# An encoder kernel: Fourier of the prompt in half the banks, opening loads in halves, later rows' norm queued behind the first rows

## Chip, core and metric

The kernel runs on one core of a Trainium2 chip. The metric is the device time of one execution in microseconds (us).

## What is computed

Two layers of a gated mixer block run over 512 positions of a prompt and 1024 of a sample, all of width 1024, in fp32. Each layer has windowed attention (8 heads), a Fourier mixing of four channel groups, gates, two merges, and an embedding that is added through a gate:

```python
for i in range(DEPTH):                       # 2 layers
    hn = rmsnorm(h, ln1[i])
    z = hn @ w_in[i]                         # 1024 -> 4352
    q, k, v, ga, uf, gf, mga, mgf = jnp.split(z, SPLIT_IDX, axis=-1)
    ...
    a = band_attention(q, k, v, sink[i]) * jax.nn.silu(ga)
    f = fourier_mix(uf, w_fmix[i]) * jax.nn.silu(gf)   # 4 groups of 128: Re(FFT2), then a 128x128 map
    merged = jax.nn.sigmoid(mga) * (a @ w_ao[i]) + jax.nn.sigmoid(mgf) * (f @ w_fo[i])
    h = h + merged @ w_out[i]
    gate = jax.nn.sigmoid(rmsnorm(h, ln_pg[i]) @ w_pg[i])
    h = h + (p[i] @ w_pe[i]) * gate
return rmsnorm(h, ln_f)
```

The prompt and the sample use the same weights.

## The kernel before

**Products.** Positions are cut into three chunks of 512 columns: chunk 0 is the prompt, chunks 1 and 2 (the pair) the sample. An activation or weight tile is split into a high part, rounded to fp32r by ScalarE (line 86), and a low part, the rest, by VectorE or GpSimd (line 87); `halves` and `hi_lo` do it. A product is then three matmuls (lines 98 to 100: high by high, high by low, low by high), each of 512 columns. The pair's input projection uses seven products in place of eight (line 233).

**Order.** The generators at the end of the kernel interleave a main stream of matmuls with a side stream (`run`). The order in the program is only a priority: a planner at compile time simulates all engines (line 1129, `schedule_with_timeline_sim=True`) and fixes, for every engine, the order in which its instructions are issued. On the chip each engine goes through that list in order and waits where an input, a buffer or a bank is not there yet. `pinned` (line 381) keeps an instruction in program order against others so marked; `normed` (line 352) doesn't.

**Stages.** First `embed(0)` multiplies the embedding input `p` by `w_pe` for all three chunks and stores the result, with `first_prompt` beside it, which loads the prompt, takes its RMS norm and makes the parts of the first projection. Then, in each layer: `project_prompt` (34 outputs of 24 matmuls, weights from `Weights`) with, beside it, the norm and the parts of the pair (`pair_normed`: rows 0 and 1 with `pinned`, rows 2 and 3 with `normed`; each row norms four tiles, then `pair_parts` makes seven split tiles of them), the prompt's attention and the prompt's Fourier part `fourier(l, 0)`; `project_pair` with the sample's attention; `merge` of the prompt with the sample's Fourier part `fourier(l, 1)` beside it; and `merge` of the pair. The last layer ends with the final norm of the pair.

**Weights.** `Weights` loads tile i+3, splits tile i+2 and hands out tile i at each step. Its `engs` names the engines of the two low parts of each tile: VectorE for the first layer's projection, GpSimd for the stream that serves both merges and the next layer's projection. In that stream tiles 0 to 23 are the prompt's merge, 24 to 47 the pair's, and those from 48 on the next projection (or, in the last layer, a second pass of gate weights).

**Banks.** PSUM has the tags mm (3 banks), sc (2), o (1) and misc (2). In `fourier(l, 0)` each group takes four banks in turn (misc, o, misc, misc) for the first transform (lines 850 to 859), each 256 columns wide, evicted by ScalarE (line 858) and VectorE (line 859), and four (sc, sc, misc, misc) for the second (line 878), of which 128 or 130 columns are used.

**Loads.** SyncE's queue issues nearly all loads. In `embed` each of the two `w_pe` tiles and each `p` tile is one transfer of 512 KB; `ln` and `ident` are loaded ahead of them.

## Time and profile before

| | us |
|---|---|
| median of 3 runs | 2255.76 (2255.22 to 2256.32) |
| the profiled execution, its own time | 2258.37 |
| its span, first to last instruction | 2255.9 |

| engine | busy, us | share of the span |
|---|---|---|
| TensorE matmul (PE) | 2182.3 | 97% |
| TensorE weight load (PEld) | 1809.5 | 80% |
| VectorE (DVE) | 1460.9 | 65% |
| ScalarE (ACT) | 1088.5 | 48% |
| GpSimd (POOL) | 558.0 | 25% |

An engine's busy time leaves out its waits and the instructions that only issue transfers. Matmuls are pipelined: a busy TensorE is not one at its peak, so stalls and the granted clock are looked for by stretch. L87 is line 87; in a tile's name the number of the buffer is left out; "out<-in" names what an instruction writes and reads.

### The profile page before, as it was taken

The page shows a single profiled execution, that of the slowest core. Times are in us where ns is not written, and L with a number is a line of the kernel's source. Part 1 is how long each engine was busy: PE and PEld are TensorE (multiplying, and loading weights), DVE is VectorE, ACT ScalarE, POOL GpSimd, SP SyncE. Part 2 cuts the span into 40 slices and gives each one's busy share as a digit, 9 for nine tenths or more (in the row PEclk, how much of TensorE's full clock was granted, in tenths as well). Part 3 has the DMA queues.
Part 4 walks back from the last instruction along what each step waited for, and adds up shares of the span by engine and source line. Part 5 has one row for each costly group of instructions (what it writes and reads, how often), then busy time and mean ns, then how long its engine had stood idle before and what let it go on. Part 6 is the DMA issues. An engine that isn't in the chain of part 4 may idle for free. (4 is left out here: it accounts for less than half of the span.)

```text
span 2255.9 us, 30026 instructions
## 1 busy us (share of the span) xinstructions
PE 2182.3 (97%) x10176; PEld 1809.5 (80%) x10176; DVE 1460.9 (65%) x2703; ACT 1088.5 (48%) x2340; POOL 558.0 (25%) x399
## 2 busy tenths in 40 slices
PE   8899999999999989999999999999999999999996
PEld 7777777788888878888888778787888888788885
DVE  5866657677667775464557564756766676864466
ACT  5477433466665454223324854336666644512342
POOL 0201100000004553312524253100000145641181
PEclk9899999999999999999999999999999999999998
DMA  7655544445448564731445554444444574653232
GB/s 279 230 181 167 188 140 163 148 137 166 150 133 294 189 236 174 251 103 51 146 158 188 173 178 167 151 165 137 143 141 158 194 270 159 225 201 117 83 118 98
DMA packets 240537, 380.69 MB, mean 169 GB/s; under 512 B 21120, under 2 KB 95488, under 8 KB 240384
## 3 DMA queue, kind: packets, MB, share of 16 engines
q1 hardware_dynamic: 233472, 366.19, 48.0%
q10 hardware_dynamic: 6912, 12.59, 1.5%
q8 instruction: 80, 1.31, 0.2%
q14 instruction: 73, 0.60, 0.1%
HBM read 270.17 MB, written 108.53 MB: 168 GB/s over the span
## 5 line engine op out<-in xcount | busy, mean ns | idle before, releaser
L233 PE MATMUL mm<-act,act 128*128 128x512 f32 x2856 | 695.2, 394 | 10.8 <-DVE scr L250 6.4
L233 PEld LDWEIGHTS mm<-act,act 128*128 128x128 f32 x2856 | 531.7, 188 | 123.4 <-issue 8.0
L98 PE MATMUL mm<-act,act 128*128 128x512 f32 x1408 | 559.1, 397 | 19.8 <-DVE scr L585 7.6
L100 PE MATMUL mm<-act,act 128*128 128x512 f32 x1408 | 556.5, 396 | 2.7 <-POOL act L87 1.3
L99 PE MATMUL mm<-act,act 128*128 128x512 f32 x1408 | 555.3, 394 | 0.0
L87 POOL TENSOR_TENSOR act<-act,act 128x512 fp32r<-128x512 f32 x284 | 404.1, 1448 | 547.2 <-ACT act L86 481.2
L86 ACT CAST act<-act 128x512 fp32r<-128x512 f32 x574 | 330.3, 619 | 225.1 <-DMA act<-in_w_af 60.7
L98 PEld LDWEIGHTS mm<-act,act 128*128 128x128 f32 x1408 | 267.8, 190 | 73.7 <-ACT act L86 13.0
L100 PEld LDWEIGHTS mm<-act,act 128*128 128x128 f32 x1408 | 267.5, 190 | 60.6 <-DVE act L87 3.5
L99 PEld LDWEIGHTS mm<-act,act 128*128 128x128 f32 x1408 | 268.1, 190 | 53.3
L87 DVE TENSOR_TENSOR act<-act,act 128x512 fp32r<-128x512 f32 x290 | 212.1, 763 | 47.1 <-ACT act L86 45.9
L87 DVE TENSOR_TENSOR act<-scr,act 128x512 fp32r<-128x512 f32 x256 | 193.7, 777 | 58.0 <-ACT act L86 56.3
L748 POOL TENSOR_TENSOR scr<-scr,scr 128x512 f32<-128x512 f32 x24 | 33.5, 1396 | 768.5 <-DVE scr L745 767.1
L86 ACT CAST act<-scr 128x512 fp32r<-128x512 f32 (+1 forms) x260 | 152.8, 615 | 144.4 <-DVE scr L410 69.0
L322 ACT ACTIVATE scr<-act 128x512 f32<-128x512 f32 x105 | 65.1, 631 | 233.7 <-DVE act L569 145.9
L87 DVE TENSOR_TENSOR act<-misc,act 128x512 fp32r<-128x512 f32 x132 | 88.1, 686 | 75.5 <-ACT act L86 75.1
L707 DVE CUSTOM_DVE_ANT_0 act<-sc,mask_sb,nsink_sb 128x384 f32<-128x384 f32 (+1 forms) x192 | 104.0, 569 | 46.4 <-PE sc L699 43.3
L710 ACT ACTIVATE act<-act,stat 128x385 f32<-128x385 f32 (+1 forms) x192 | 110.5, 578 | 43.9 <-DVE stat L707 43.4
L86 ACT CAST act<-misc 128x512 fp32r<-128x512 f32 x132 | 73.8, 586 | 106.8 <-PE misc L734 104.9
L98 PE MATMUL sc<-act,act 128*128 128x512 f32 (+1 forms) x292 | 111.1, 381 | 0.0
L100 PE MATMUL sc<-act,act 128*128 128x512 f32 (+1 forms) x292 | 110.6, 379 | 0.0
L99 PE MATMUL sc<-act,act 128*128 128x512 f32 (+1 forms) x292 | 110.5, 379 | 0.0
(207 smaller groups left out, 2642.8 us busy)
## 6 DMA issues: line engine op xcount, KB each, us to landing
act<-in_w_in SPq DMA_DIRECT2D x136, 256.0 KB, 4.5
act<-in_w_in SPq DMA_DIRECT2D x68, 512.0 KB, 4.8
gt<-scr SPq DMA_DIRECT2D x96, 256.0 KB, 2.3
scr<-gt SPq DMA_DIRECT2D x96, 256.0 KB, 5.3
act<-in_w_pg SPq DMA_DIRECT2D x80, 256.0 KB, 3.8
act<-in_w_af SPq DMA_DIRECT2D x64, 256.0 KB, 5.3
act<-in_w_out SPq DMA_DIRECT2D x64, 256.0 KB, 5.4
pl<-scr ACTq DMA_DIRECT2D x48, 256.0 KB, 2.5
```

What stands on the lines that cost most here:

```text
L86: S.copy(hi, src)
L87: lo_eng.tensor_tensor(lo, src, f(hi), op=ALU.subtract)
L98: PE.matmul(out, wh, xh, start=i == 0, stop=False)
L99: PE.matmul(out, wh, xl, start=False, stop=False)
L100: PE.matmul(out, wl, xh, start=False, stop=i == n - 1)
L233: PE.matmul(bank, w, v, start=first and k == 0 and n == 0, stop=k == 3 and n == 2, skip_group_check=True)
L322: S.activation(sq, h, AF.Square)
L707: V.tensor_tensor_reduce(out=pr[:, :W], in0=sc[:, :W], in1=msk, scale=-0.125, scalar=nsink_sb[:, l, head : head + 1], op0=ALU.add, op1=ALU ...
L710: S.activation(pr, pr, AF.Exp, bias=nmx[:, e], scale=-1.0, accum_out=rs[:, e])
L748: G.tensor_tensor(a2, a2, gate, op=ALU.mult)
```

## The change

Six edits are made together:

- `embed`: the two `w_pe` tiles are loaded in halves, with the halves of `p`'s first tile between them, ahead of `ln` and `ident`; all low parts are made by VectorE (before, half of the `w_pe` ones by GpSimd); in layer 0 its products go round six banks in place of three.
- Opening: the first two weight tiles of the first projection are loaded behind the prompt's `x`, and split after some of the prompt's parts, in a generator `opening` that runs beside `embed(0)`.
- `pair_normed`: the norm of rows 2 and 3 is queued on VectorE behind the last subtraction of the row before.
- `fourier(l, 0)`: both halves of a first transform share one bank, and are evicted together; the four sums of the second transform share two banks.
- `Weights`: the engines of the low parts depend on the tile's place in the stream: VectorE for tiles 0 to 23, GpSimd for 24 to 47, VectorE from 48 on.

```diff
--- before.py
+++ after.py
@@ -106,12 +106,7 @@
             pass
 
 
-    def const(src, shape, name):
-        t = cpool.tile(shape, F32, tag=name, name=name)
-        SY.dma_start(t, src)
-        return t
-
-    ln_sb = const(ln, [P, 5, KD], "ln_sb")
+    ln_sb = cpool.tile([P, 5, KD], F32, tag="ln_sb", name="ln_sb")
     mean_sb = cpool.tile([P, 1], F32, tag="mean_sb", name="mean_sb")
     V.memset(mean_sb, 1.0 / D)
     ident_sb = cpool.tile([P, P], F32, tag="ident_sb", name="ident_sb")
@@ -160,7 +156,7 @@
         def split(self, i):
             if i < len(self.sources):
                 self.w[i] = []
-                for r, eng in zip((slice(0, 4), slice(4, 8)), self.engs):
+                for r, eng in zip((slice(0, 4), slice(4, 8)), self.engs[min(i // 24, 2)]):
                     t = wt([P, 2, 4, P], F32R)
                     hi_lo(t[:, 0], t[:, 1], self.raw[i][:, r], eng)
                     self.w[i] += [(t[:, 0, k, :], t[:, 1, k, :]) for k in range(4)]
@@ -371,7 +367,7 @@
         yield
         x["B21"].append(two(halves(b21, V)))
         yield
-        V.tensor_tensor(b21, b21, t2, op=ALU.subtract)
+        x["last"] = V.tensor_tensor(b21, b21, t2, op=ALU.subtract).ins
         x["T4"].append(two(halves(b21, V)))
         yield
         x["B22"].append(two(halves(b22, V)))
@@ -386,7 +382,11 @@
             hs = [[tile(i, kk) for i in range(2)] for kk in (k, k + 4)]
             for j in range(2):
                 for i in range(2):
-                    (pinned if k < 2 else normed)(hs[j][i], k + 4 * j, gain, rbs[i])
+                    if k < 2:
+                        pinned(hs[j][i], k + 4 * j, gain, rbs[i])
+                    else:
+                        with tc.issue_after(x["last"]):
+                            normed(hs[j][i], k + 4 * j, gain, rbs[i])
                 yield
             yield from pair_parts(x, hs[0][0], hs[0][1], hs[1][0], hs[1][1])
 
@@ -628,18 +628,25 @@
             SY.dma_start(raw, p[l, c].rearrange("k p t -> p k t"))
             return raw
 
-        ws, raws = {}, []
+        ws, raws = {}, [big([P, 2, T]) for _ in range(2)]
+        raws_p = [big([P, 2, T])]
+
         for k in range(2):
-            raws.append(big([P, 2, T]))
-            SY.dma_start(raws[-1], w_pe[l, k].rearrange("p (i d) -> p i d", i=2))
-            if k == 0:
-                raws_p = [load(0), load(1)]
-        yield
+            SY.dma_start(raws[k][:, 0, :], w_pe[l, k, :, 0:T])
+            SY.dma_start(raws_p[0][:, k, :], p[l, 0, k])
+        for k in range(2):
+            SY.dma_start(raws[k][:, 1, :], w_pe[l, k, :, T:])
+        if l == 0:
+            SY.dma_start(ln_sb, ln)
+            SY.dma_start(ident_sb, ident)
+        raws_p.append(load(1))
+        yield
+        ts = []
         for i in range(2):
             for k in range(2):
-                ws[k, i] = halves(raws[k][:, i, :], V if k else G)
-                if i + k == 0:
-                    ts = [halves(raws_p[0][:, j, :], V) for j in range(2)]
+                ws[k, i] = halves(raws[k][:, i, :], V)
+                if i == 0:
+                    ts.append(halves(raws_p[0][:, k, :], V))
         yield
         for c in range(NCH):
             parts = [two(t) for t in ts]
@@ -650,7 +657,7 @@
                 if m == 4 and c + 1 < NCH:
                     ts = [halves(raws_p[c + 1][:, k, :], V) for k in range(2)]
                 o = slice(m % 4 * P, m % 4 * P + P)
-                out = pst("mm")
+                out = any_ps() if l == 0 else pst("mm")
                 mm3(out, [(ws[k, m // 4][:, 0, o], ws[k, m // 4][:, 1, o]) for k in range(2)], parts)
                 a = scr()
                 S.copy(a, out)
@@ -847,14 +854,18 @@
             for i in range(2):
                 a = scr()[:, : 2 * n * P]
                 for par in range(2):
-                    pm = pst(("misc", "o", "misc")[(2 * i + par) % 3])
+
+                    if s or par == 0:
+                        pm = pst(("misc", "o", "misc")[(2 * i + par) % 3] if s else "misc")
                     for t in range(n):
-                        j, lo = 2 * t * P, 2 * t * P + par
+                        j, lo = (2 * t if s else 2 * par) * P, 2 * t * P + par
                         uh, ul = (z[:, lo : lo + 2 * P - 1 : 2] for z in us[i])
                         PE.matmul(pm[:, j : j + 2 * P], uh, cw[i][:, :, gs], start=True, stop=False)
                         PE.matmul(pm[:, j : j + P], ul, cw[i][:, 0, gs], start=False, stop=True)
-                    pv = pm[:, : 2 * n * P].rearrange("p (t h d) -> p t h d", t=n, h=2)
-                    av = a[:, par * n * P : (par + 1) * n * P].rearrange("p (t d) -> p t d", t=n)
+                    if s == 0 and par == 0:
+                        continue
+                    pv = pm.rearrange("p (t h d) -> p t h d", t=2, h=2)
+                    av = (a[:, par * n * P : (par + 1) * n * P] if s else a).rearrange("p (t d) -> p t d", t=2)
                     S.copy(av, pv[:, :, 1])
                     V.tensor_tensor(av, av, pv[:, :, 0], op=ALU.add)
                 yield
@@ -875,7 +886,11 @@
             if g < 3:
                 folded = fold(u)
             yield
-            acc = [pst("sc"), pst("sc"), pst("misc"), pst("misc")]
+            if s:
+                acc = [pst("sc"), pst("sc"), pst("misc"), pst("misc")]
+            else:
+                b0, b1 = pst("sc"), pst("sc")
+                acc = [b0, b0[:, 2 * P :], b1, b1[:, 2 * P :]]
             for i in range(4):
                 a, par = ab[i // 2], i % 2
                 wx = [(a[:, 0, (par * n + t) * P :][:, :P], a[:, 1, (par * n + t) * P :][:, :P]) for t in range(n)]
@@ -976,14 +991,21 @@
     def w_ins(l):
         return [w_in[l, m] for m in range(NMT)]
 
-    SY.dma_start(ident_sb, ident)
     parts, tiles, rbs = [], [], []
-    first = first_prompt(parts)
-    run(embed(0), [(first, 1, 0.7)])
-    late_constants()
-    ws = Weights(w_ins(0), (V, V))
-    for _ in ws.start():
-        pass
+    ws = Weights(w_ins(0), ((V, V),) * 3)
+
+    def opening():
+        first, weights = first_prompt(parts), ws.start()
+        next(first)
+        next(weights)
+        late_constants()
+        yield
+        for n, _ in enumerate(first):
+            if n == 12:
+                next(weights, None)
+            yield
+
+    run(embed(0), [(opening(), 1, 0.7)])
     for l in range(DEPTH):
         last = l == DEPTH - 1
         xs = {n: [] for n in ("B11", "T2", "T1", "T3", "B21", "T4", "B22")}
@@ -1008,7 +1030,7 @@
         ])
         for _ in pair_made(xs, l, range(3, 4)):
             pass
-        ws = Weights(streams(l) + ([] if last else w_ins(l + 1)), (G, G))
+        ws = Weights(streams(l) + ([] if last else w_ins(l + 1)), ((V, V), (G, G), (V, V)))
         fx = {c: [] for c in range(NCH)}
         run(project_pair(l, xs, pairs, ws.start()), [
             (chain(attention(l, PAIR, True), mixed(0, range(8), fx)), 14 * 5, 1.4),
```

## Rows read from the trace of the kernel before

**Rows 1.** The page, part 1: busy us, share of the span, instructions.
```profile
PE 2182.3 (97%) x10176; PEld 1809.5 (80%) x10176; DVE 1460.9 (65%) x2703; ACT 1088.5 (48%) x2340; POOL 558.0 (25%) x399
```

**Rows 2.** Waits of PE, whole span: total us, times, longest us.
```profile
PE misc L328 <- DVE scr L323: 8.2, 3, 6.3
```

**Rows 3.** Stretches: busy us (instructions) by engine, PEclk granted, DMA share, GB/s.
```profile
15.00:40.00 25.00, 25.00 (x117) 20.80 (x116) 15.52 (x33) 17.69 (x34) 0.00 (x0) 1.00 0.67 235
...
104.04:111.69 7.65, 6.53 (x15) 4.66 (x16) 6.93 (x12) 4.09 (x8) 0.00 (x0) 0.50 0.90 275
234.60:241.40 6.80, 6.80 (x24) 6.12 (x25) 4.56 (x23) 3.25 (x12) 0.59 (x1) 0.50 0.31 112
831.90:838.70 6.80, 3.46 (x8) 2.81 (x9) 5.88 (x9) 1.89 (x3) 1.32 (x1) 0.50 0.11 42
1340.50:1347.30 6.80, 6.36 (x17) 5.18 (x18) 3.31 (x15) 2.09 (x8) 2.07 (x3) 0.50 0.20 74
```

**Rows 4.** Timeline of the opening: start, us, engine, line, tiles [idle before, releaser].
```profile
0.74 0.39 SPq L111 DMA_DIRECT2D ln_sb<-in_ln  x1
...
1.65 0.42 SPq L634 DMA_DIRECT2D act<-in_w_pe  x1
...
5.21 0.62 ACT L86 CAST act<-act 128x512 fp32r<-128x512 f32 x1 [3.19 <-DMA act<-in_w_pe]
6.71 1.14 ACT L86 CAST act<-act 128x512 fp32r<-128x512 f32 x2 [0.89 <-DMA act<-in_p]
...
7.38 1.65 PE L98 MATMUL mm<-act,act 128*128 128x512 f32 x3 [7.38 <-ACT act L86]
```

**Rows 5.** Timeline of DVE while the pair's rows are normed, layer 0.
```profile
94.06 2.73 DVE L352 SCALAR_TENSOR_TENSOR act<-act,ln_sb,scr 128x512 f32<-128x512 f32 x4
...
98.03 2.73 DVE L352 SCALAR_TENSOR_TENSOR act<-act,ln_sb,scr 128x512 f32<-128x512 f32 x4
...
103.22 1.88 DVE L455 SCALAR_TENSOR_TENSOR scr<-scr,mm 128x512 f32<-128x512 f32 x3
...
105.61 1.28 DVE L87 TENSOR_TENSOR act<-act,act 128x512 fp32r<-128x512 f32 x2
```

**Rows 6.** Timeline of PE in the same stretch.
```profile
104.04 0.76 PE L98 MATMUL mm<-act,act 128*128 128x512 f32 x1 [4.58 <-DVE scr L455]
...
106.35 0.80 PE L100 MATMUL mm<-act,act 128*128 128x512 f32 x1 [1.12 <-DVE act L87]
```

**Rows 7.** Timeline of ACT, DVE and PE in the prompt's Fourier part, layer 0.
```profile
231.19 1.81 ACT L86 CAST act<-act 128x512 fp32r<-128x512 f32 x3 [1.09 <-DMA act<-in_w_in]
...
231.84 2.51 DVE L87 TENSOR_TENSOR act<-act,act 128x512 fp32r<-128x512 f32 x3 [0.92 <-ACT act L86]
...
234.60 0.58 PE L854 MATMUL misc<-act,scr 128*128 128x256 f32 x1 [2.76 <-DVE scr L859]
```

**Rows 8.** Waits of PE from 1305 to 1350 (the same part, layer 1).
```profile
PE misc L98 <- ACT scr L86: 1.1, 1, 1.1
PE misc L100 <- DVE scr L87: 1.1, 1, 1.1
```

**Rows 9.** Timeline of POOL, DVE and PE where the first prompt merge ends.
```profile
820.30 12.91 POOL L87 TENSOR_TENSOR act<-act,act 128x512 fp32r<-128x512 f32 x8 [4.70 <-issue]
...
827.00 3.43 DVE L87 TENSOR_TENSOR act<-act,act 128x512 fp32r<-128x512 f32 x2
...
833.69 0.68 DVE L347 COPY scr<-misc 128x512 f32<-128x512 f32 x1
...
835.24 0.77 PE L98 MATMUL mm<-act,act 128*128 128x512 f32 x1 [5.90 <-DVE scr L585]
```

**Rows 10.** POOL's groups in 680 to 836: busy us, mean ns | idle before.
```profile
L87 POOL TENSOR_TENSOR act<-act,act 128x512 fp32r<-128x512 f32 x48 | 69.7, 1479 | 61.6 <-ACT act L86 41.4 <-DMA act<-in_w_pg 6.2 <-issue 4.7
```

**Rows 11.** Stretches of the first prompt merge, columns as in Rows 3.
```profile
680.00:836.00 156.00, 150.10 (x754) 127.43 (x753) 117.87 (x210) 78.56 (x160) 87.91 (x61) 0.99 0.70 250
...
720.00:760.00 40.00, 40.00 (x221) 34.66 (x221) 36.38 (x72) 18.25 (x42) 25.91 (x18) 1.00 0.75 269
```

## Prediction, made before the change was run

> **What bounds the kernel now.** The first view is the page's busy times: TensorE is busy 97% of the span [rows 1], no other engine over 80%. So time is won only where TensorE waits or runs at its lower clock, and the second view, its list of waits, says where. Its largest entry, 8.2 us before the norm's sums, is mostly one wait of 6.3 at the very end [rows 2], which no edit touches; that leaves 1.9. The third view, the table by stretches, gives what a matmul costs: 117 in 25.0 us at a granted clock of 1.00, so 0.21 us each, and there are stretches at 0.50, which is 1.2 instead of 2.4 GHz [rows 3]. Each of these lies behind a stretch in which TensorE stood still or nearly so, and it costs about half its length. A stall's price is therefore the wait and the slow stretch behind it. Last come the timelines around the three largest stalls which the edits reach.
>
> **Opening: 2.5 us.** The first `w_pe` tile is issued at 1.65, as the third transfer; its cast starts 3.56 us later, that of `p` at 6.71, and the first matmul at 7.38, 0.67 behind it [rows 4]. After the change a half of `w_pe` takes the place of `ln` at 0.74, and a half of `p` follows at about 1.2 (one issue is 0.39 to 0.42). If the halves take as long as the whole tile did, the casts start at 4.30 and 4.92 (one cast is 0.62) and the first matmul at 5.6: 1.8 us earlier. If half the bytes take half the time (1.78), the casts are at 2.5 and 3.1 and the matmul at 3.8: 3.6 earlier. I take 2.5, nearer to the first, since part of a transfer's time doesn't shrink with its size. From 15 to 40 TensorE is busy 25.0 of 25.0 us [rows 3], so a shift of the start shifts the end of this stage, provided that the first projection's weights are there earlier too. The edit loads these behind `x`, as four more transfers on SyncE's queue (4 times 0.4 us of issue); if they came no earlier than before, the term would be 0. Splitting the weights costs VectorE nothing more than before, and moving half of the `w_pe` low parts there from GpSimd costs two times 0.64 (a pair takes 1.28 [rows 5]) while it has little else. The six banks in place of three I cost at nothing, as TensorE has no gap from 15 us on. Range: 0 to 3.6.
>
> **Norm of rows 2 and 3: 8 us.** Between 94.06 and 100.7 VectorE runs eight `normed` instructions, in two groups of 2.73 us [rows 5], though rows 2 and 3 are wanted far later. Behind them stand the three instructions of line 455 at 103.22, which empty the three mm banks. TensorE waits for the first of these from 99.46 to 104.04, for a low part 1.12 more, and runs at 0.50 until 111.69 [rows 3, 6]. From 99.46 to 111.69 are 12.2 us with 15 matmuls, worth 3.2: 9.0 are lost. Queued behind the first rows' last subtraction, the eight leave this place, and VectorE's list moves up by 5.4. Line 455 then starts at 97.8, ahead of 99.46: that wait is gone. The low part of 105.61, whose first instruction ends near 106.25, comes at 100.85, while TensorE wants it after two matmuls, at 99.9: about 1 us stays. That is too little to expect a slow stretch, so 8 are won. If the slow stretch came all the same (7.65 us at half speed cost 15 times 0.2, so 3.0), 5 would be won; at most it is 9. The eight instructions don't vanish: four come behind row 1, four behind row 2, both in the prompt's projection with attention and Fourier beside it. VectorE is idle 35% of the span [rows 1], so I cost them at nothing; without this cover they are 5.4. In layer 1 no wait of TensorE lies at this place, and I expect nothing.
>
> **Prompt's Fourier part: 4 us, both layers together.** In layer 0 a first-transform matmul waits 2.76 us for the bank which line 859 empties, and 6.80 us at 0.50 follow [rows 3, 7]: 2.8 + 3.4 = 6.2. In layer 1 there are two waits of 1.1 and 6.80 us at 0.50 [rows 3, 8]: 5.6. With both halves of a transform in one bank, two banks are taken where four were, so the wait for line 859 has no cause any more. But the timeline shows why line 859 was late: VectorE had three low parts ahead of it (2.51 us), ScalarE their casts, and both waited for weights from memory [rows 7]. The second transform needs the same evictions, so its matmuls can wait in place of the first's. The two waits of layer 1 are for such parts, not for a bank. I take a third of 11.8, so 4. The bounds are 11.8 won, and 4 lost if the larger common eviction makes the chain longer (a wait of 1.1 more in two groups of each layer). One ScalarE and one VectorE instruction fewer per transform are off the path.
>
> **Low parts on VectorE: 3.5 us at the merge, 1.5 elsewhere.** While GpSimd makes eight low parts (820.30 to 833.2), VectorE's pair takes 3.43 us, another like it lasts to 833.69, and the norm's copy waits behind both [rows 9]. Alone a pair takes 1.28 [rows 5]. So two GpSimd instructions beside it lengthen a pair by 2.15, two pairs by 4.3. TensorE waits 5.90, and then runs 8 matmuls in 6.80 us at 0.50 [rows 3, 9]; from 829.34 to 838.7 are 9.4 us for 1.7 of work: 7.7 lost. With GpSimd quiet the 4.3 come back, but up to eight low parts move into VectorE's list (8 times 0.64 = 5.1), some of them ahead of the copy. I take the slow stretch alone (3.4, rounded 3.5): the wait shrinks to where the clock stays up. Bounds: 7.7 won, 5.1 lost. In the whole merge, of GpSimd's 48 low parts [rows 10] 42 are weights (four make tables and two the next embedding): 42 times 0.64 = 27 us more on VectorE, where 117.9 of 156 are busy [rows 11]. That fits on the mean. The prompt's merge of layer 1, the second projection and the last gate weights are changed alike; I put 1.5 down for them, most of the 1.9 of the norms' waits, whose sums GpSimd shares [rows 2]. Bounds: 3 either way.
>
> **A rule that speaks against the Fourier edit.** No row shows two sums in one bank. The Trainium skill, in "PSUM — Partial Sum Buffer", The four PSUM rules, says that two accumulation groups which are open at once in the same bank can't both begin with a clearing matmul. So the second sum must start when the first is complete, its low part included; a rival below prices that.
>
> **Sum.** 2.5 + 8 + 4 + 3.5 + 1.5 = 19.5 us, from a span of 2255.9: 2236.4. The profiled execution took 2258.37, 2.5 more than its span; the median of the runs, 2255.76, is 0.1 below the span, so I forecast 2236. About 0.2%, 4.5 us, is what a measurement of this kernel can tell from no change.
>
> **Rivals.**
> - *VectorE becomes the bound in the prompt's merges (slower).* From 720 to 760 it is busy 36.4 of 40 us [rows 11]. An even share of the 42 low parts is 10.8 there, 6.9 us: 43.3 of 40, so 3.3 late, if GpSimd's silence returns nothing. With 5.1 at the merge's end and a slow stretch of 3.4 behind each, that is 15.2 a layer, 30.4 in both; with opening and norm kept, 2255.8 - 10.5 + 30.4 = 2276. It turns the sign once TensorE waits over 10.5 us for low parts. Against it: the 2.15 a pair gives back. Chance 0.08.
> - *The waits move on.* The slow stretch behind the norm stays (5 won), the opening gives 1.8, Fourier and merge nothing: 2249. For it: the low part of 105.61 and the weights of [rows 7] are next in line. Chance 0.16.
> - *Sums one after the other.* The second sum waits for the first's low part, 1.1 us [rows 8] in each of 8 groups: 8.8 lost and the 4 not won: 2236 + 12.8 = 2249. Chance 0.06.
> - *The change doesn't do what it says.* The planner orders all engines anew, and its list brings as many new waits as leave: 2256, within 3. Chance 0.10.
> - *Every stall goes in full.* 3.6 + 9 + 11.8 + 7.7 + 1.9 = 34: 2222. Chance 0.10.
>
> **How the numbers follow.** The forecast, 2229 to 2245, has 0.50. The range 2223 to 2251 leaves out the fourth rival and the first (0.18). Faster by over 0.2% (below 2251.2) are the forecast, the last rival and most of the second and third: 0.80. Within 0.2%: 0.12, slower 0.08.
>
> **What would show it.** Right: the first matmul near 4.9; no wait near 99 and no clock of 0.50 there, and line 352 behind line 374; no wait of line 854 for line 859; VectorE's pairs at 1.3 us near 827. Wrong: VectorE at 39 of 40 us in the sample's Fourier part with TensorE waiting for line 87; the second transform waiting in place of the first; the normed rows in a new gap of TensorE near 130 or 300.

## The result, and the profile after

The changed kernel takes 2232.16 us (median; 2228.84 to 2233.25) against 2255.49 of the kernel before on the same chip (2254.18 to 2256.32): 0.9895 of it, with an interval of 0.9877 to 0.9912. That is 23.3 us less, where 19.5 were forecast. The profiled execution took 2233.25 us, its span is 2231.5, 24.4 below the span before.

The first line of the page, kernel after (it answers to [rows 1]; busy us, share of the span, instructions):

```profile
PE 2172.4 (97%) x10176; PEld 1803.0 (81%) x10176; DVE 1500.9 (67%) x2871; ACT 1087.7 (49%) x2324; POOL 297.3 (13%) x215
```

TensorE's 10176 matmuls are the same, with 10 us less of busy time, since less of it lies at the low clock. GpSimd has handed 184 instructions away and lost 261 us, VectorE has gained 168 and only 40 us: on balance its other instructions became shorter.

**Where the time went** is read by setting the start of the n-th matmul of the two traces side by side (worked out from the matmuls' starts, n counted from 0; us):

```
n-th matmul       before    after   difference
first                7.4      5.2     2.2
200                 54.5     52.4     2.1
380                 94.8     93.3     1.5
400                104.0     97.9     6.1
420                113.1    103.8     9.2
900                212.9    204.2     8.8
1100               258.7    241.5    17.2
3700               813.7    797.5    16.2
3800               842.9    823.9    18.9
6000              1325.1   1305.5    19.6
6300              1392.2   1370.4    21.8
9900              2173.0   2150.7    22.3
last              2244.9   2220.3    24.6
```

Five places carry it: 2.2 at the start (0.7 of it is gone by 95 us), 7.3 at the pair's norm, 8.4 in the prompt's Fourier part of layer 0 and 2.2 in that of layer 1, 2.7 where the first prompt merge ends. What is left is about 2.4, and the last part, behind n = 9900, has 2.3 of it.

Line numbers have moved: 348 is `normed` (352 before), 370 the first rows' last subtraction (374), 863 the first transform's matmul (854), 870 its eviction (859), 319 and 324 the norms' sums (323, 328), 343 the norm's copy (347). Lines 86, 87, 98 to 100, 455 and 585 have kept their numbers.

The opening, ACT and PE, kernel after (start, us, engine, line, tiles; answers to [rows 4]):

```profile
3.57 0.62 ACT L86 CAST act<-act 128x512 fp32r<-128x512 f32 x1 [1.56 <-DMA act<-in_w_pe]
4.50 1.96 ACT L86 CAST act<-act 128x512 fp32r<-128x512 f32 x3 [0.31 <-DMA act<-in_p]
...
5.17 0.79 PE L98 MATMUL sc<-act,act 128*128 128x512 f32 x1 [5.17 <-ACT act L86]
```

The cast comes 2.83 us after the half's issue at 0.74, where the whole tile took 3.56: half the bytes took 0.8 of the time. The half is also the first transfer of the queue, where the whole tile was the third, so size and place aren't told apart.

The pair's norm, DVE, kernel after (answers to [rows 5]):

```profile
91.92 2.73 DVE L377 SCALAR_TENSOR_TENSOR act<-act,ln_sb,scr 128x512 f32<-128x512 f32 x4
...
97.10 1.28 DVE L455 SCALAR_TENSOR_TENSOR scr<-scr,mm 128x512 f32<-128x512 f32 x2
...
116.89 0.69 DVE L370 TENSOR_TENSOR act<-act,scr 128x512 f32<-128x512 f32 x1
117.50 2.74 DVE L348 SCALAR_TENSOR_TENSOR act<-act,ln_sb,scr 128x512 f32<-128x512 f32 x4
```

PE in the same stretch (answers to [rows 6]):

```profile
99.64 0.50 PE L100 MATMUL mm<-act,act 128*128 128x512 f32 x1 [1.01 <-DVE act L87]
```

No `normed` of the later rows stands between 91.92 and 97.10; the first four come right behind line 370, the other four at 253.41. Line 455 starts at 97.10, where it was at 103.22, and of TensorE's waits only the one for the low part is left, 1.01.

TensorE's waits from 76 to 235, kernel after (us in all, times, longest):

```profile
PE o L746 <- ACT act L86: 1.5, 1, 1.5
PE sc L706 <- DVE stat L714: 1.2, 2, 0.9
PE misc L324 <- DVE scr L319: 1.1, 1, 1.1
PE mm L100 <- DVE act L87: 1.0, 1, 1.0
PE misc L863 <- DVE act L87: 0.3, 1, 0.3
...
```

The wait of 2.76 for the eviction [rows 7] is gone and nothing of its size stands in its place: the two largest that are left belong to the prompt's attention.

Stretches of the kernel after (columns as in [rows 3]; the first four lie where those of [rows 3] lay, the last two answer to [rows 11]):

```profile
99.00:112.00 13.00, 12.37 (x53) 9.79 (x54) 12.31 (x21) 6.26 (x12) 0.00 (x0) 1.00 0.71 232
205.00:232.00 27.00, 26.58 (x150) 22.92 (x151) 23.64 (x75) 17.97 (x51) 8.20 (x9) 1.00 0.80 268
816.80:820.10 3.30, 3.30 (x9) 2.52 (x9) 2.43 (x4) 1.30 (x3) 0.00 (x0) 0.50 0.24 89
1318.50:1325.30 6.80, 6.52 (x19) 5.54 (x20) 3.58 (x19) 1.96 (x8) 1.97 (x2) 0.50 0.21 80
664.00:820.00 156.00, 153.01 (x761) 129.21 (x760) 130.12 (x256) 79.90 (x162) 26.05 (x17) 0.99 0.71 251
704.00:744.00 40.00, 40.00 (x222) 34.77 (x221) 38.08 (x85) 18.18 (x42) 8.39 (x5) 1.00 0.75 269
```

Norm and layer 0's Fourier part run at 1.00 throughout; the stretch at 0.50 behind the merge is 3.4 long in place of 6.8; the one in layer 1's Fourier part has stayed. In the merge VectorE has 12.2 us more than before and is busy 38.1 of 40 us in its densest part, and TensorE still 40.00 of 40.

The end of the first prompt merge, DVE, kernel after (answers to [rows 9]):

```profile
810.36 1.29 DVE L87 TENSOR_TENSOR act<-scr,act 128x512 fp32r<-128x512 f32 x2
...
814.76 0.69 DVE L343 COPY scr<-misc 128x512 f32<-128x512 f32 x1 [0.81 <-PE misc L341]
```

TensorE's waits there, from 810 to 822, kernel after:

```profile
PE mm L98 <- DVE scr L585: 1.7, 1, 1.7
PE misc L341 <- DVE tiny L335: 1.3, 1, 1.3
```

A pair of low parts takes 1.29 where it took 3.43; GpSimd does nothing from 795 to 818. The norm's copy now waits for TensorE itself, not behind low parts. TensorE waits 3.0 in all where it waited 5.90 [rows 9]. The stretch at 0.50 behind it is half as long, but it still holds 9 matmuls, where it held 8 [rows 3]: what was won here is the wait, not the slow stretch.

### The profile page after: what moved, and what is told of

It is laid out like the page before. It is cut to its first block, busy times and chain, and to the rows that moved or that the text cites. A ratio compares the mean times of both kernels' runs of the same rounds, so it can differ in the third digit from the quotient of the medians.

```text
span 2231.5 us, 29985 instructions
## 1 busy us (share of the span) xinstructions
PE 2172.4 (97%) x10176; PEld 1803.0 (81%) x10176; DVE 1500.9 (67%) x2871; ACT 1087.7 (49%) x2324; POOL 297.3 (13%) x215
## 5 line engine op out<-in xcount | busy, mean ns | idle before, releaser
L229 PE MATMUL mm<-act,act 128*128 128x512 f32 x2856 | 694.4, 393 | 11.8 <-DVE scr L246 6.5
L229 PEld LDWEIGHTS mm<-act,act 128*128 128x128 f32 x2856 | 530.9, 188 | 124.1 <-ACT act L86 9.1
L98 PE MATMUL mm<-act,act 128*128 128x512 f32 x1384 | 545.9, 395 | 3.6 <-DVE scr L585 3.3
L100 PE MATMUL mm<-act,act 128*128 128x512 f32 x1384 | 544.2, 394 | 2.9 <-DVE act L87 2.8
L99 PE MATMUL mm<-act,act 128*128 128x512 f32 x1384 | 543.4, 393 | 0.0
L87 DVE TENSOR_TENSOR act<-act,act 128x512 fp32r<-128x512 f32 x474 | 332.1, 735 | 32.4 <-ACT act L86 30.8
L100 PEld LDWEIGHTS mm<-act,act 128*128 128x128 f32 x1384 | 261.5, 189 | 59.9 <-DVE act L87 6.4
L98 PEld LDWEIGHTS mm<-act,act 128*128 128x128 f32 x1384 | 261.8, 189 | 55.7 <-issue 3.7
L99 PEld LDWEIGHTS mm<-act,act 128*128 128x128 f32 x1384 | 261.7, 189 | 52.0
L87 DVE TENSOR_TENSOR act<-scr,act 128x512 fp32r<-128x512 f32 x256 | 180.5, 727 | 56.3 <-ACT act L86 55.1
L87 POOL TENSOR_TENSOR act<-act,act 128x512 fp32r<-128x512 f32 x100 | 142.5, 1450 | 324.9 <-ACT act L86 274.5
L87 DVE TENSOR_TENSOR act<-misc,act 128x512 fp32r<-128x512 f32 x132 | 88.2, 686 | 74.1 <-ACT act L86 73.8
L98 PE MATMUL sc<-act,act 128*128 128x512 f32 (+1 forms) x308 | 118.0, 383 | 5.2 <-ACT act L86 5.2
L100 PE MATMUL sc<-act,act 128*128 128x512 f32 (+1 forms) x308 | 117.1, 380 | 0.0
L99 PE MATMUL sc<-act,act 128*128 128x512 f32 (+1 forms) x308 | 117.0, 380 | 0.0
```

The lines of the kernel that those rows point to most:

```text
L87: lo_eng.tensor_tensor(lo, src, f(hi), op=ALU.subtract)
L98: PE.matmul(out, wh, xh, start=i == 0, stop=False)
L99: PE.matmul(out, wh, xl, start=False, stop=False)
L100: PE.matmul(out, wl, xh, start=False, stop=i == n - 1)
L229: PE.matmul(bank, w, v, start=first and k == 0 and n == 0, stop=k == 3 and n == 2, skip_group_check=True)
```

## The experiments

**One part of the change undone at a time.** The kernel before beside these four: 2256.9. The change itself was not run again beside them, so the differences below are from its 2232.2; from the ratios to the kernel before they come out as 7.2, 11.7, -0.7 and 12.4.

*The norm's rows 2 and 3 free again:*

```diff
-                    if k < 2:
-                        pinned(hs[j][i], k + 4 * j, gain, rbs[i])
-                    else:
-                        with tc.issue_after(x["last"]):
-                            normed(hs[j][i], k + 4 * j, gain, rbs[i])
+                    (pinned if k < 2 else normed)(hs[j][i], k + 4 * j, gain, rbs[i])
```

> The changed kernel (2232.2 us) with the norm of rows 2 and 3 free again to go ahead; all else as changed. Theory: these eight VectorE instructions stand ahead of the ones that empty the mm banks, so the wait near 99 us and the stretch at a clock of 0.50 behind it come back; the n-th matmul of the two traces shows 7.0 us won there, so this run takes 2239 (2237 to 2242). Rival, the waits only move on (a low part is late anyway): 1 to 3 us, so 2233 to 2235. Rival, the new order of the planner alone: any time from 2228 to 2236, with no wait for line 455.

Measured: 2240.18 (2237.83 to 2241.58), 0.9927 of before (0.9914 to 0.9939): 8.0 above the change. DVE and PE of this kernel (line 451 is 455 of the change):

```profile
93.28 2.73 DVE L348 SCALAR_TENSOR_TENSOR act<-act,ln_sb,scr 128x512 f32<-128x512 f32 x4
...
97.26 2.73 DVE L348 SCALAR_TENSOR_TENSOR act<-act,ln_sb,scr 128x512 f32<-128x512 f32 x4
...
103.27 0.77 PE L98 MATMUL mm<-act,act 128*128 128x512 f32 x1 [5.26 <-DVE scr L451]
```

The stretch behind:

```profile
102.98:109.81 6.83, 5.43 (x12) 3.87 (x13) 6.11 (x11) 3.31 (x8) 0.00 (x0) 0.50 0.82 275
```

The eight return to their old place, with them the wait (5.26) and the stretch at 0.50, and the n-th matmul falls 7.6 us behind the changed kernel between n = 390 and 410. At the end of the two traces 5.9 are left. The mechanism is shown; the size is 6 to 8.

*The Fourier part in as many banks as before* (both transforms):

```diff
-                    if s or par == 0:
-                        pm = pst(("misc", "o", "misc")[(2 * i + par) % 3] if s else "misc")
+                    pm = pst(("misc", "o", "misc")[(2 * i + par) % 3])
...
-            if s:
-                acc = [pst("sc"), pst("sc"), pst("misc"), pst("misc")]
-            else:
-                b0, b1 = pst("sc"), pst("sc")
-                acc = [b0, b0[:, 2 * P :], b1, b1[:, 2 * P :]]
+            acc = [pst("sc"), pst("sc"), pst("misc"), pst("misc")]
```

> The changed kernel with the prompt's Fourier part in as many banks as before. Theory, banks: matmuls wait for line 859's eviction again; the traces show 8 us won at this place in layer 0 and 2 in layer 1, so 2242 (2239 to 2245). Rival, the second transform waits in place of the first, so that the gain there came from the other edits' new order: 2230 to 2235.

Measured: 2244.71 (2241.74 to 2246.82), 0.9947 (0.9933 to 0.9961): 12.5 above the change. Waits of PE from 200 to 245, this kernel (line 862 is the first transform):

```profile
PE o L862 <- ACT scr L86: 1.3, 1, 1.3
PE misc L862 <- DVE act L87: 0.9, 1, 0.9
```

A stretch there:

```profile
217.80:224.60 6.80, 6.10 (x15) 4.65 (x16) 6.45 (x20) 6.61 (x17) 1.19 (x1) 0.50 1.00 369
```

The stretch at 0.50 is back in layer 0, and the n-th matmul falls from 1.8 (n = 900) to 9.0 (n = 1080) us behind there, and from 9.0 (n = 5900) to 10.9 (n = 6300) in layer 1. But the waits ahead of it are for casts and low parts of the transform's input; none is for the eviction. So the edit is worth what its whole stall was worth, though the list doesn't name a bank.

The order of the instructions does show the shortage. The third and the fourth part of the first group's first transform, PE, this kernel:

```profile
208.17 0.39 PE L862 MATMUL misc<-act,scr 128*128 128x256 f32 x1
...
214.58 0.28 PE L862 MATMUL misc<-act,scr 128*128 128x256 f32 x1
```

The same two in the kernel after:

```profile
206.34 0.38 PE L863 MATMUL misc<-act,scr 128*128 128x256 f32 x1
206.62 0.34 PE L863 MATMUL misc<-act,scr 128*128 128x256 f32 x1
```

With four banks the fourth part stands 6.4 us behind the third, with matmuls of the projection between them (from 215.09 to 221.53 in the kernel before); with the change it stands 0.28 behind. A bank that isn't free in the plan is planned around, and so appears as an order and not as a wait. This fits the edit, but isn't shown to be all: in this kernel the first part's bank was empty at 210.46, and the fourth part stands 4.1 us behind that. The planner's reasons aren't on record.

*The opening as before:*

```diff
         for k in range(2):
-            SY.dma_start(raws[k][:, 0, :], w_pe[l, k, :, 0:T])
-            SY.dma_start(raws_p[0][:, k, :], p[l, 0, k])
...
+            raws.append(big([P, 2, T]))
+            SY.dma_start(raws[-1], w_pe[l, k].rearrange("p (i d) -> p i d", i=2))
+            if k == 0:
+                raws_p = [load(0), load(1)]
...
-                out = any_ps() if l == 0 else pst("mm")
+                out = pst("mm")
...
```

This is a part of the diff. `ln` and `ident` at the head of the queue, the `w_pe` low parts shared with GpSimd and the first weights behind `embed` are as before too.

> The changed kernel with the opening as before: whole w_pe tiles, ln and ident first, weights after embed, embed in three mm banks. Theory: the first matmul is at 7.4 instead of 5.2 us and nothing later makes it up: 2234.4 (2233.5 to 2236). Rival, a shift at the start is taken up by the waits for the pair's norm near 77 us: 2232.

Measured: 2232.11 (2230.42 to 2232.73), 0.9892 (0.9878 to 0.9905): no difference from the change. The matmuls are 2.36 us behind at the start, 2.26 at n = 120, 1.29 at n = 310 (77 us), 0.56 at n = 410. The gain is there, and 1.7 of it are given back at the pair's norm; from n = 1900 on this kernel is the one ahead, by 2.3 at the end.

*GpSimd makes the low parts of the merges' weights again:*

```diff
-        ws = Weights(streams(l) + ([] if last else w_ins(l + 1)), ((V, V), (G, G), (V, V)))
+        ws = Weights(streams(l) + ([] if last else w_ins(l + 1)), ((G, G),) * 3)
```

> The changed kernel with all low parts of the merge stream on GpSimd again. Theory: GpSimd's low parts lengthen VectorE's where the first prompt merge ends, and the wait there comes back as a part: 2.7 us at that place, with 1 to 2 elsewhere: 2236 (2234 to 2239). Rival, VectorE has the time and the gain came from the new order: 2232. Rival, the low parts cost VectorE more than they give: 2225 to 2231.

Measured: 2243.81 (2242.91 to 2248.86), 0.995 (0.9937 to 0.9962): 11.6 above the change. PE where layer 1's attention begins, this kernel:

```profile
1223.12 0.74 PE L706 MATMUL sc<-act,scr 128*128 128x256 f32 x4 [3.59 <-DMA scr<-q]
```

The merge's end costs 3.3 (n = 3700 to 3800), and there is a wait that the forecast didn't name: the first scores wait 3.59 us for the load of `q`, and the clock falls behind it; the matmuls go from 5.2 to 11.6 behind between n = 5550 and 5710.

**The halves of the two large parts.** The kernel before beside these four: 2256.18.

*First transforms in four banks, the sums still share:* the part of the Fourier diff above its `...`.

> The changed kernel, with each half of a first transform in a bank of its own as before (misc, o, misc, misc); the four sums still share two sc banks. Undoing both took 2244.7 against 2232.2. Theory, the freed misc banks: as the sums no longer hold misc, the fourth half finds a bank soon, and most of the gain stays: 2234 to 2238. Rival, the count of four banks per group is what blocks, whoever holds the others: 2241 to 2246, with waits for line 859's eviction.

*Sums in four banks, the transforms still share:* the part below it.

> The changed kernel, with the four sums in sc, sc, misc, misc as before; the halves of a first transform still share a bank. Theory, the freed misc banks: the first transforms of the next group must wait until the last two sums are read, so most of the gain goes: 2238 to 2244. Rival, the halves' shared bank is what counts: 2232 to 2235.

Measured: 2241.53 (2236.17 to 2246.57), 0.9933 (0.992 to 0.9947), and 2242.09 (2239.01 to 2244.24), 0.9937 (0.9923 to 0.995). Either half undone costs some 9.5 of the 12.5; the two don't add. Without the other each is worth 2.6 to 3.2, no more than two plans differ by (below), so that may be nothing. That sharing sums alone free enough banks for the first transforms (2234 to 2238) falls. In both a stretch at 0.50 is back in layer 0's Fourier part, at 215.9 and at 223.7. The order of the first transforms differs in each: with them in four banks the fourth part of the first group comes 7.0 us behind the first (205.69 to 212.69; 0.9 with the change); with the sums in four banks a group's parts stay together, but the second group's begin 13.8 behind the first's (203.53 to 217.30; 8.5 with the change). So each half delays the transforms in another way; why a slow stretch follows stays open.

*Low parts on VectorE for the prompt's merges alone:*

```diff
-        ws = Weights(streams(l) + ([] if last else w_ins(l + 1)), ((V, V), (G, G), (V, V)))
+        ws = Weights(streams(l) + ([] if last else w_ins(l + 1)), ((V, V), (G, G), (G, G)))
```

> The changed kernel with low parts on VectorE only for tiles 0 to 23 (the prompt's merges), on GpSimd from 48 on (the second projection, the last gate weights). All on GpSimd took 2243.8, the change 2232.2. By the offsets of the traces, the end of the first prompt merge gives 2.7 to 5 of that, and the second projection with attention and Fourier most of the rest: 2237 to 2241. Rival, the prompt's merges give nearly all, the second projection nothing, as forecast: 2232 to 2235.

Measured: 2239.47 (2236.81 to 2241.82), 0.9925 (0.9913 to 0.9938). So the prompt's merges are worth 2243.8 - 2239.5 = 4.3, and the second projection with the last gate weights 7.3 (5.6 and 6.7 from the ratios). The forecast had 3.5 and 1.5. The traced execution is the fastest of the five (2236.81): it ends 3.6 behind the change, and loses 3.7 between n = 5540 and 5710, where TensorE waits 2.5 us for the load of `q`.

*All low parts on VectorE:*

```diff
-        ws = Weights(streams(l) + ([] if last else w_ins(l + 1)), ((V, V), (G, G), (V, V)))
+        ws = Weights(streams(l) + ([] if last else w_ins(l + 1)), ((V, V),) * 3)
```

> The changed kernel with tiles 24 to 47 (the pair's merges) on VectorE too, so that no weight's low part is left to GpSimd. Theory: GpSimd's low parts cost TensorE only where it waits for VectorE, and in the pair's merges it doesn't wait, so 2230 to 2233. Rival, 48 more low parts make VectorE the bound there: over 2236.

Measured: 2239.12 (2237.0 to 2242.96), 0.9928 (0.9915 to 0.994), 7 above the change. Its time is the rival's, its trace isn't: from 830 to 2170 us the matmuls stay 3 to 5 us behind, and the distance doesn't grow, so TensorE loses nothing in the pair's merges, where VectorE got the work. What is lost lies at the merge's end, in layer 0's Fourier part, and in one wait at the very end (PE, this kernel):

```profile
2224.96 1.20 PE L324 MATMUL misc<-mean_sb,scr 128*128 128x1 f32 x5 [13.27 <-DVE scr L319]
```

It was 6.5 with the change. The cause stands one norm earlier (DVE, this kernel):

```profile
2182.31 0.17 DVE L328 TENSOR_SCALAR misc<-misc 128x4 f32<-128x4 f32 x1 [5.57 <-PE misc L324]
```

VectorE waits 5.57 us for the matmuls of line 324, which the plan sets behind more products here (at 2181.33, though their input is done at 2176.7); with the change it waits 1.21. All of VectorE's work behind comes 9.7 later, the last sums too. So this is the plan, not VectorE's load. The traced execution is also the slowest of the five (2242.96), so these 6.8 us are shown for it and not for the median.

**What gives the opening back.** The trace points at the norm's sums near 77 us, which VectorE and GpSimd share. So the first pair's sums go to VectorE alone, with the new opening and with the old one:

```diff
-                ns[i].add(us[i, k], V if (k + i) % 2 else G)
+                ns[i].add(us[i, k], V)
```

> The changed kernel, with the sums of squares of the pair's first norm all on VectorE (before, every other one on GpSimd). Theory: the opening's 2.2 us are given back from 77 us on because this chain of sums, in which VectorE and GpSimd lengthen each other's instructions (1.78 instead of 0.68), doesn't come as much earlier as the matmuls; without GpSimd it ends some 4 us earlier, the wait of 1.3 near 77 goes, and the opening's gain stays: 2229 to 2231. Rival, the chain is bound by ScalarE's squares: no change, 2231 to 2233.

> The same, with the opening as before the change. Without the edit to the sums, undoing the opening took 2232.1, as the change (2232.2). Theory: with the wait near 77 gone, the opening is worth its 2.2 us, so this is 2 to 2.5 slower than the run with the sums alone. Rival, the later parts give the opening back in any case: the two are equal within 1 us.

Measured: 2229.8 (2227.78 to 2230.44), 0.9883 (0.9868 to 0.9897), and 2231.37 (2229.61 to 2232.96), 0.9891 (0.9878 to 0.9903), with the kernel before at 2255.37. Timeline of DVE, POOL and PE near the sums, kernel after:

```profile
61.41 0.68 DVE L319 TENSOR_TENSOR scr<-scr,scr 128x512 f32<-128x512 f32 x1
...
64.96 1.78 DVE L319 TENSOR_TENSOR scr<-scr,scr 128x512 f32<-128x512 f32 x1
...
67.26 1.78 DVE L319 TENSOR_TENSOR scr<-scr,scr 128x512 f32<-128x512 f32 x1
...
63.20 2.99 POOL L319 TENSOR_TENSOR scr<-scr,scr 128x512 f32<-128x512 f32 x2
66.88 1.61 POOL L319 TENSOR_TENSOR scr<-scr,scr 128x512 f32<-128x512 f32 x1 [0.69 <-DVE scr L319]
...
74.34 2.37 DVE L319 TENSOR_TENSOR scr<-scr,scr 128x512 f32<-128x512 f32 x2 [1.19 <-POOL scr L319]
...
76.25 1.58 POOL L319 TENSOR_TENSOR scr<-scr,scr 128x512 f32<-128x512 f32 x1 [0.70 <-DVE scr L319]
...
76.86 2.08 PE L324 MATMUL misc<-mean_sb,scr 128*128 128x1 f32 x16 [1.13 <-DVE scr L319]
```

The same with the sums on VectorE alone (new opening):

```profile
68.92 4.89 DVE L319 TENSOR_TENSOR scr<-scr,scr 128x512 f32<-128x512 f32 x8
...
75.35 0.95 PE L324 MATMUL misc<-mean_sb,scr 128*128 128x1 f32 x8
```

With the change the sums hand over from one engine to the other and end at about 78. On VectorE alone they end at 73.8, the matmul waits for nothing, no stretch at 0.50 follows near 79, and the matmuls are 3.2 us ahead of the change by n = 330. Between the two kernels of this pair the opening's 2.4 us are 2.3 past the sums (n = 380) and 2.2 at the end of the traces, though not steadily: 6.0 at n = 1500, 1.9 at 6300. The medians differ by 1.6, and their runs overlap. So where the gain is first lost is shown by the traces; how much is kept in the median isn't. At 2229.8 the first of them has the lowest median of all, but its interval overlaps the change's.

**What a plan without a price does.** The second set of the next weights is asked for two steps earlier in the opening, which no term prices:

```diff
-            if n == 12:
+            if n == 10:
```

> The changed kernel with the first projection's weights split two steps earlier in the opening (at step 10 instead of 12); nothing else. No theory gives this a price, so it shows what a new plan alone does: theory, under 2 us either way (2230 to 2234). Rival, new plans scatter by as much as the parts of this change: over 4 us away.

Measured: 2235.54 (2230.03 to 2242.46), 0.9912 (0.9898 to 0.9927): 3.4 above the change, between the two expectations, and spread over 12 us. So a difference of up to 3 or 4 us between two plans is not yet the worth of an edit: this bears on the opening and the sums, on the 4.3 of the prompt's merges and on what one Fourier half is worth alone; less on 8, 11.6 and 12.5.

**The norm's edit alone, on the kernel before:**

```diff
-                    (pinned if k < 2 else normed)(hs[j][i], k + 4 * j, gain, rbs[i])
+                    if k < 2:
+                        pinned(hs[j][i], k + 4 * j, gain, rbs[i])
+                    else:
+                        with tc.issue_after(x["last"]):
+                            normed(hs[j][i], k + 4 * j, gain, rbs[i])
```

> The kernel before with the norm of rows 2 and 3 queued behind the rows before, and nothing else. Theory: its price doesn't depend on the other edits: undone in the changed kernel it cost 8.0 us, so alone it gives 7 to 9 from 2255.5 to 2256.9: 2247 to 2249. Rival, part of the 8 needs the low parts or the opening: 2250 to 2253.

Measured: 2256.32 (2252.92 to 2259.24) beside 2255.37, 1.0003 (0.9995 to 1.0012): nothing. Its matmuls win 8.3 by n = 420, 11.7 by n = 1050, and have 8.4 left at n = 3790, behind the merge's end. Between n = 5550 and 5570, where layer 1's attention begins, they lose 6.7, and the last 1.5 at n = 5990, in layer 1's Fourier part. SP's waits there, from 1190 to 1234, this kernel (line 281 stores gates, line 459 is 455 of the change):

```profile
SPq L281 <- DVE scr L459: 24.9, 4, 8.8
```

The timeline of SP and PE at that place:

```profile
1220.69 0.33 SPq L281 DMA_DIRECT2D gu<-scr  x1
...
1223.11 0.97 SPq L682 DMA_DIRECT2D scr<-q  x2
...
1228.60 1.22 PE L703 MATMUL sc<-act,scr 128*128 128x256 f32 x4 [3.79 <-DMA scr<-q]
```

The stretch behind:

```profile
1227.71:1234.54 6.83, 5.95 (x16) 4.88 (x17) 0.92 (x4) 1.09 (x4) 0.25 (x1) 0.50 1.10 351
```

The loads of `q` stand in SyncE's queue behind stores of gates, and those wait for VectorE. In the kernel before the same load is issued at 1227.76, hidden since TensorE arrives later; here the load has come 4.7 us earlier and TensorE 8.4. The load itself is also slower: the fastest of `q`'s loads takes 5.4 us from issue to landing, 3.8 in the kernel before, with the DMA engines busy 0.96 of the time from 1224.0 to 1228.6. With the whole change it is far ahead of its use (SP, kernel after; TensorE comes to it at about 1216):

```profile
1203.11 0.33 SPq L277 DMA_DIRECT2D gu<-scr  x1
1203.54 1.54 SPq L685 DMA_DIRECT2D scr<-q  x3
```

Of all the kernels here, TensorE waits for `q` at this place in three: this one, GpSimd with all low parts (3.59) and GpSimd with those from tile 48 on (2.5). These are the ones that have the norm's edit and leave the second projection's low parts to GpSimd. So the norm's 8 us reach the end only where these low parts are VectorE's. That the stores' place in the queue is what holds the load is read from the timelines; no run moved the loads ahead of them. It also says for the larger part why the four undone parts sum to 8.0 + 12.5 + 0.0 + 11.6 = 32.1 and the change to 23.3: undoing the low parts counts this wait (6.4 in its trace), which the kernel before, with neither of the two edits, doesn't have. The other 2.4 are within what two plans differ by. The edit's order of VectorE also moved four normed rows from 1197.2 to 1221.7 there; their share in the late stores wasn't tried apart.

## Why the prediction was right, step by step

The forecast, 2236 with 2229 to 2245 as its own range, held: 2232. It held as a sum better than by its terms, and that was in part luck: the opening's 2.5 came to nothing at the end, the Fourier part and the low parts elsewhere were put 8.5 and 5.8 too low, and 8.8 of the undone parts' worth didn't add. The sentence on the range 2223 to 2251 also leaves out that the last rival, at 2222, lies outside it.

- **Opening, 2.5 forecast.** At its own place right: the first matmul 2.2 earlier (5.17; 4.9 forecast), the casts (3.57, 4.50) between the two bounds. Right to the end it was not: undoing it costs nothing. The step that failed is "a shift of the start shifts the end of this stage", read from the stretch 15 to 40, where TensorE never waits. It should have been read on to the next wait, the norm's sums near 77, whose chain on VectorE and GpSimd ends only 1.3 earlier than with the opening undone (77.84 against 79.13).
- **Norm, 8 forecast.** 7.3 in the trace, 8.0 when undone: right in mechanism and near in size. Line 455 at 97.1 (97.8 forecast), 1.01 left for the low part (about 1 forecast), and no stretch at 0.50. "In layer 1 ... I expect nothing" and "I cost them at nothing" hold for the change as a whole; for the edit alone they don't, because the time won takes away the cover of the load of `q`. The forecast looked for a new wait at the norm's place in layer 1, not at the next transfer that TensorE would overtake.
- **Prompt's Fourier part, 4 forecast.** The term that was mis-sized: 12.5 when undone, 8.4 and 2.2 in the trace, against an upper bound of 11.8. "I take a third" was the step that failed. In layer 0 the whole stall went (6.2 was put on it), the stretch at 0.50 included, and more with it: TensorE's waits there from 200 to 245 were 4.7 in all, not 2.76 alone, and 0.5 are left; the fear that the second transform waits in place of the first didn't come true. In layer 1 the stretch stayed, behind a wait for the input's cast, as the forecast said; but its list for layer 1 [rows 8] shows two of five entries, and one that it leaves out, 0.7 us in two waits, is for line 859, so a bank was short there too. The reason given was half right: no wait for the eviction is left, but with the banks undone the recorded waits name casts and low parts, and the shortage appears in the order; half of the edit does little by itself.
- **Low parts, 3.5 and 1.5 forecast.** 3.5 at the merge's end against 2.7 in the trace, and 4.3 for the prompt's merges when the rest is left: near in size. The pairs are at 1.29 as expected, but the step to the time wasn't: the 3.5 was the slow stretch, since "the wait shrinks to where the clock stays up". The wait shrank, from 5.9 to 3.0, and the clock fell all the same, for 9 matmuls in place of 8. The 1.5 "elsewhere" was the wrong size, 7.3 when undone, and for another reason than the norms' waits that were named (1.9 before without the last one, 1.6 after). Where a trace shows it, it lies at the load of `q`, which no row of the forecast showed as a wait, because before the change it was none.
- **VectorE as the bound.** Priced at 3.3 us in the densest part. VectorE came to 38.1 of 40 us there, not to the 43.3 of that rival, and TensorE waited for nothing. In the whole merge VectorE got 12.2 us more, where 27 were estimated: GpSimd's silence paid for the rest.
- **Sums one after the other.** No wait of this kind stands in the list from 76 to 235. What would happen without that order was not tried.
- **The plan.** That the planner orders everything anew was given as a rival with 3 us either way. The kernel with one number changed moved by 3.4, near that size. A new wait in the place of one that left is also what undid the norm alone.
- **Every stall in full** was summed to 34; the undone parts come near it with 32.1, but 8.8 of that don't add: 6.4 are the load of `q`, the rest isn't assigned.

## What to carry to other kernels

A microsecond won on the bounding engine is won only up to the next thing that doesn't move with it: follow the shift through the later stages, and look for the transfer or the chain on other engines that was just hidden before. A load that stands in a queue behind stores is issued only when these are (four of them waited 24.9 us here), so its due time is read from its queue, not from its size. A bank that is short may appear as an order of the instructions and not as a wait. Undo the parts one at a time and also try one alone: parts that share a later wait can each be worth much when undone, and nothing when made alone, as the norm was here.

## What was not expected of the hardware

**A wait of the same size has or hasn't a slow stretch behind it.** The same matmul of the same stage, timeline of PE, in the kernel before:

```profile
339.65 1.85 PE L233 MATMUL mm<-act,act 128*128 128x512 f32 x5 [2.63 <-DVE scr L250]
```

Its stretch behind:

```profile
340.40:343.70 3.30, 3.30 (x9) 2.59 (x8) 3.27 (x5) 0.00 (x0) 1.58 (x1) 0.50 0.03 10
```

In the kernel after, the matmul and the stretch behind it:

```profile
322.78 3.88 PE L229 MATMUL mm<-act,act 128*128 128x512 f32 x16 [2.50 <-DVE scr L246]
```

```profile
323.00:326.40 3.40, 3.40 (x16) 2.80 (x16) 3.37 (x6) 0.00 (x0) 1.58 (x1) 1.00 0.09 36
```

Nine matmuls in 3.3 us at a granted clock of 0.50 (1.2 GHz) against 16 in 3.4 at 1.00 (2.4 GHz), behind waits of 2.63 and 2.50; in layer 1 of the kernel after a wait of 2.04 was followed by 6.8 us at 0.50. That is 1.5 to 3 us that hang on little, and may be a part of the spread of equal kernels; the traces don't show what decides.

**VectorE beside GpSimd.** The addition of two 128x512 tiles took 0.68 where it started first (61.41) and 1.78 where GpSimd's was already running. Both that are shown ended 0.55 us behind GpSimd's (66.74 against 66.19, 69.04 against 68.49), so VectorE's seems to have stood until GpSimd's was done. Shared, a round of two additions took 2.3 us (64.96 to 67.26), where VectorE alone made eight in 4.89, so two in 1.2. That dividing such a chain between the two engines lost time here is shown by these rows. The Trainium skill, in "SBUF — State Buffer", Who interferes with whom, says that a VectorE instruction with both inputs in SBUF contends with a GpSimd instruction that reads it; the rows agree (1.78 against 0.68).
